# Preparation of the token mixers in pools of their own, ahead of the embedding block

## The chip, the cores and the metric

One Trainium2 chip, one of its cores. The time is device microseconds from start to end of one execution of the whole program; the median of several runs is given. A core has five engines with queues of their own: TensorE (PE, matmuls), VectorE (DVE), ScalarE (ACT), GpSimd (POOL) and SyncE (SP, here only for starting transfers).

## The reference

One step of a four-layer streaming encoder on 256 prompt tokens and 64 sample tokens (320 columns, `NT`), model width 1024, float32. The mixers of the layers are: latent attention (layer 0), stick-breaking attention (1), sliding-window attention (2), latent attention (3). Per layer:

```
x += mixer(rms_norm(x, g_mix))          # with caches of past keys and values for the sample
x += conv_ffn(rms_norm(x, g_ffn))       # 1024 -> 2 x 2816 -> conv of 3 tokens, gelu, gate -> 1024
x += sigmoid(rms_norm(x, g_ple) @ w_gate) * (p[i] @ w_proj)      # the embedding block
```

and a last `rms_norm`. The new keys, values, latents and conv states are outputs too. The caches depend on no layer's result: latents and rotary keys of 256 past tokens, stick-breaking keys and values of 256, window keys and values of 128.

## The kernel before

Everything lies transposed: a feature tile is 128 partitions by 320 token columns. Each float32 operand of PE is kept as a rounded high part and a low part, the remainder, and each product is three matmuls (`mm3`, L190 to L193): high x high, low x high, high x low. `split` (L147 to L150) makes the two parts: ACT copies to the rounded type, DVE (or POOL) subtracts.

The weights are one stream of 450 chunks of eight 128x128 tiles, in the order of use. `fetch` (L157) starts a chunk's transfer on SP's queue, then ACT makes `whi` and DVE `wlo`; inside a mixer every second (window attention: every third) chunk's `wlo` goes to POOL (`wpool`, L164). `take` keeps two chunks ahead (`WAHEAD`); raw chunks have 3 buffers, split chunks 4. Layer 0 takes chunks 0 to 122, layer 1 to 230, layer 2 to 326, layer 3 to 449; a fetch runs two chunks ahead of the use.

A norm is spread over the code: `norm_piece` (L286 on) makes x·g in two parts and adds up the squares, chunk by chunk, as x becomes final; `norm_finish` sums over the partitions with PE (`col_sums`, L261), makes the factor with eleven small DVE steps (`newton_rsqrt`, L241 to L247), and spreads it over the partitions with DVE (L271, L272), PE (L276) and ACT (L279: the tile R). Products with x·g can start before; their results are multiplied by R as they leave PSUM. PSUM has 3 banks for "mm", 3 for "sc", 2 for "tp".

`run` opens a pool `mix{i}` per mixer and a pool `ffn{i}` for `ffn_ple`, the feed-forward part and the embedding block. Each pool takes the memory of the one closed before it. A pool that is opened over a closed one waits, at its first use, for all of the closed one's work. The mixers begin with preparation that needs no x: `mla` loads the rotary table, the cached latents `ckt` and the rotary keys, splits them, clears tiles; `sba` loads the constants `cst`, clears the block-diagonal query tiles `BD`, and per head pair loads and splits a cache `kc`; `swa` loads its rotary table, and in `keys` and `vals` its caches.

The order of instructions on each engine is not the order of the code: a planner that simulates the engines takes, among the instructions whose inputs are ready in its simulation, the earliest in the code. On the chip every engine then goes through its queue in that fixed order, and an instruction that waits holds up all behind it.

Of the kernel before, what the change touches and what calls it, by code (L numbers as in the profile page):

```python
# [8 lines left out]
F32 = mybir.dt.float32  # L9
# [3 lines left out]
ALU = mybir.AluOpType  # L13
# [34 lines left out]
# Order of the 64 rotary features on the partitions: halves interleaved by 16,  # L48
# so that a rotation partner lies in the same quadrant of 32 partitions.
# [55 lines left out]
class Kernel:  # L105
# [16 lines left out]
    # -- small helpers --  # L122
# [29 lines left out]
    # -- weights --  # L152
# [4 lines left out]
    def fetch(self, c):  # L157
# [6 lines left out]
        e = nc.gpsimd if self.wpool and c % self.wpool == 0 else nc.vector  # L164
# [3 lines left out]
    def take(self, name, rows, cols):  # L168
        """The next 128x128 weight tile of the stream, as (high, low) parts."""
# [10 lines left out]
    def take_wide(self, name, rows, cols):  # L180
        """Several tiles of the stream side by side."""
# [13 lines left out]
    def proj(self, out, name, cols, xs, rows=None):  # L195
        """out[cols, tokens] = W[:, cols]^T x over the K tiles xs."""
# [13 lines left out]
    # -- constants, inputs --  # L210
# [54 lines left out]
    def spread(self, r, pool, tag, bufs=2):  # L265
        """A [128, 3] column per token, to every partition: [128, NT]."""
# [19 lines left out]
    def norm_piece(self, m):  # L286
        """Chunk m of x is final: its squares, and x*g in two parts."""
# [47 lines left out]
    # -- the feed-forward block and the per-layer embedding --  # L335
    def ffn_ple(self, i, pool, after):
        nc, tc = self.nc, self.tc
# [3 lines left out]
        pT = self.tile(pool, [P, 2, NT], "pT")  # L341
        nc.sync.dma_start(out=pT, in_=self.t["pT"][i])
        a = []
        for j in range(NF):
# [3 lines left out]
            # gate with the two earlier tokens: zeros and prompt, conv state and sample  # L348
# [29 lines left out]
        ph = self.tile(pool, [P, 2, NT], "pTh", F32R)  # L378
        pl = self.tile(pool, [P, 2, NT], "pTl", F32R)
# [3 lines left out]
        self.norm_start(f"g_ple{i}", pool, "ph")  # L383
        for m in range(NK):
            p = self.ps(("mm", "sc")[m % 2])
            self.proj(p[:, 0:NT], f"fout{i}", np.arange(m * P, m * P + P), a)
            self.add_x(m, p, True)
        h = self.norm_finish(pin=PINS[4])
# [26 lines left out]
    # -- rotary embedding of psum (scaled already if src is SBUF) --  # L415
# [16 lines left out]
    # -- multi-head latent attention --  # L432
    def mla(self, j, pool):
# [8 lines left out]
        flat = lambda x: x.rearrange("p a b -> p (a b)")  # L442
        tmp2, krt, *tmp = (flat(T([P, 2, 3 * P], f"PT{x}", bufs=2)) for x in "hlhl")
        krt = krt[:, 0:W]
        tmp = [x[:, o:o + NT] for x in tmp for o in (0, NT)]
        ckt = T([P, 2, W], "ckt")
        q = nc.sync
        q.dma_start(out=ckt[:, :, NT:W], in_=t["ckvT"][j])
        q.dma_start(out=krt[:, NT:W], in_=t["krT"][j])
# [920 lines left out]
```

## Time and profile before

| | |
|---|---|
| median of 3 runs | 1863.24 us (1861.02 to 1864.79) |
| profiled execution | span 1860.9 us; the time around the span is not given |
| PE busy | 1787.0 us, 12352 matmuls |
| DVE, ACT, POOL busy | 1349.1, 973.4, 568.1 us |
[...]
| transfers | 254.15 MB, mean 137 GB/s |

The span is the time from the first to the last instruction. "Idle before" an instruction is the time for which its engine had nothing running, with the instruction that ended the wait. Matmuls overlap in their engine, so a matmul's duration is longer than the distance to the next.

### The profile page before, as it was taken

How to read it: one execution, taken by the hardware profiler on the slowest of the kernel's cores; microseconds unless marked ns; L12 is line 12 of the kernel's file. 1: busy time of each engine (PE TensorE's matmuls, PEld its weight loads, DVE VectorE, ACT ScalarE, POOL GpSimd, SP SyncE). 2: the span in 40 equal slices, each digit the busy share in tenths (PEclk: the TensorE clock that was granted, in tenths of full speed). 3: DMA queues.
4: the chain of work that ended last, by engine and by line, in shares of the span. 5: the costliest groups of instructions: out<-in, count | busy, mean ns of one | idle time of the engine just before them, and what ended most of it. 6: DMA issues, size and time to landing. Idle time of an engine off the chain costs nothing.

```text
span 1860.9 us, 32664 instructions
## 1 busy us (share of the span) xinstructions
PE 1787.0 (96%) x12352; PEld 1768.3 (95%) x12352; DVE 1349.1 (72%) x2627; ACT 973.4 (52%) x1841; POOL 568.1 (31%) x834
## 2 busy tenths in 40 slices
PE   7999999999989999999997999999979999999996
PEld 6899999999989999999997999999979999999996
DVE  7977687764778888774589787764778777877546
ACT  5776654433558854444457654433547675444332
POOL 3333343321132234330045143321243334333103
PEclk9999999999989999999998999999989999999998
DMA  6333344444443334444352144444432333444441
GB/s 210 106 110 121 121 137 165 152 149 147 148 147 131 126 132 148 148 157 150 125 181 80 58 148 162 147 153 147 138 123 98 128 126 129 150 148 158 149 147 63
DMA packets 78126, 254.15 MB, mean 137 GB/s; under 512 B 9488, under 2 KB 18192, under 8 KB 77968
## 3 DMA queue, kind: packets, MB, share of 16 engines
q1 hardware_dynamic: 77248, 251.34, 38.9%
q8 instruction: 97, 1.59, 0.3%
q10 hardware_dynamic: 720, 0.71, 0.1%
q14 instruction: 61, 0.50, 0.1%
HBM read 243.55 MB, written 5.85 MB: 134 GB/s over the span
## 4 chain that ended last, share of the span: by engine, by line
PE 85%; DVE 7%; ACT 4%; issue 2%; DMA 1%; POOL 1%; DVEq 0%; SPq 0%; ACTq 0%; POOLq 0%
PE ps L191 27%; PE ps L192 27%; PE ps L193 27%; ACT whi L163 1%; DVE wlo L165 1%; DVE rsh L546 1%; DMA wraw<-w 1%; ACT Pr L625 1%; PE ps L645 1%; PE ps L261 0%; PE ps L592 0%; PE ps L593 0%; DVE nb L623 0%; PE ps L1065 0%; PE ps L276 0%
## 5 line engine op out<-in xcount | busy, mean ns | idle before, releaser
L163 ACT ACTIVATE whi<-wraw 128x1024 fp32r<-128x1024 f32 x450 | 474.1, 1056 | 432.5 <-PE ps L192 220.7
L165 DVE TENSOR_TENSOR wlo<-wraw,whi 128x1024 fp32r<-128x1024 f32 x381 | 472.8, 1241 | 228.2 <-ACT whi L163 221.8
L165 POOL TENSOR_TENSOR wlo<-wraw,whi 128x1024 fp32r<-128x1024 f32 x69 | 166.8, 2418 | 287.5 <-ACT whi L163 275.5
L368 POOL TENSOR_TENSOR ge<-cv,R 128x256 f32<-128x256 f32 (+1 forms) x176 | 132.9, 774 | 92.6 <-ACT cv L365 92.2
L309 POOL TENSOR_TENSOR acc<-acc,sq 128x320 f32<-128x320 f32 x72 | 77.4, 1074 | 260.7 <-ACT sq L303 259.8
L331 DVE TENSOR_TENSOR x<-x,ps 128x320 f32<-128x320 f32 x128 | 61.2, 483 | 53.4 <-PE ps L193 53.1
L363 DVE SCALAR_TENSOR_TENSOR cv<-G,cols,cv 128x322 f32<-128x322 f32 x176 | 96.0, 553 | 2.4
L372 DVE TENSOR_TENSOR af<-ge,ps 128x320 f32<-128x320 f32 x88 | 42.8, 486 | 67.7 <-POOL ge L368 67.4
L191 PE MATMUL ps<-h0hi,whi 128*128 128x320 f32 x256 | 81.5, 319 | 8.0 <-ACT h0hi L294 6.5
L191 PE MATMUL ps<-h4hi,whi 128*128 128x320 f32 x256 | 79.9, 314 | 1.1 <-ACT h4hi L149 1.1
L192 PE MATMUL ps<-h0lo,whi 128*128 128x320 f32 x256 | 80.1, 313 | 0.8 <-DVE h0lo L295 0.8
L192 PE MATMUL ps<-h5lo,whi 128*128 128x320 f32 x256 | 79.5, 311 | 1.2 <-DVE h5lo L150 1.2
L192 PE MATMUL ps<-h3lo,whi 128*128 128x320 f32 x256 | 80.3, 314 | 0.0
L191 PE MATMUL ps<-h2hi,whi 128*128 128x320 f32 x256 | 80.2, 313 | 0.0
L192 PE MATMUL ps<-h2lo,whi 128*128 128x320 f32 x256 | 80.2, 313 | 0.0
L191 PE MATMUL ps<-h3hi,whi 128*128 128x320 f32 x256 | 80.1, 313 | 0.0
L193 PE MATMUL ps<-h3hi,wlo 128*128 128x320 f32 x256 | 80.1, 313 | 0.0
L191 PE MATMUL ps<-h1hi,whi 128*128 128x320 f32 x256 | 80.0, 312 | 0.0
L193 PE MATMUL ps<-h1hi,wlo 128*128 128x320 f32 x256 | 79.9, 312 | 0.0
L192 PE MATMUL ps<-h1lo,whi 128*128 128x320 f32 x256 | 79.9, 312 | 0.0
L193 PE MATMUL ps<-h0hi,wlo 128*128 128x320 f32 x256 | 79.9, 312 | 0.0
L193 PE MATMUL ps<-h2hi,wlo 128*128 128x320 f32 x256 | 79.8, 312 | 0.0
(793 smaller groups left out, 6516.3 us busy)
## 6 DMA issues: line engine op xcount, KB each, us to landing
wraw<-w SPq DMA_DIRECT2D x450, 512.0 KB, 3.2
QR<-rsh SPq DMA_DIRECT2D x32, 80.0 KB, 2.0
kc<-sbc SPq DMA_DIRECT2D x8, 256.0 KB, 3.0
x<-xT SPq DMA_DIRECT2D x8, 160.0 KB, 4.1
pT<-pT SPq DMA_DIRECT2D x4, 320.0 KB, 3.3
o_sbk<-kvf SPq DMA_DIRECT2D x8, 160.0 KB, 1.8
o_sbv<-kvf SPq DMA_DIRECT2D x8, 160.0 KB, 1.8
cossin<-rot SPq DMA_DIRECT2D x3, 384.0 KB, 3.2
```

The lines of the kernel that those rows point to most:

```text
L163: nc.scalar.activation(out=hi, in_=raw, func=AF.Copy)
L165: e.tensor_tensor(out=lo, in0=raw, in1=hi.bitcast(F32), op=ALU.subtract)
L191: mm(out, w[0], x[0], start=first, stop=False, **kw)
L192: mm(out, w[0], x[1], start=False, stop=False, **kw)
L193: mm(out, w[1], x[0], start=False, stop=last, **kw)
L309: e.tensor_tensor(out=self.nacc[:, 0:NT], in0=self.nacc[:, 0:NT], in1=sq, op=ALU.add)
L331: self.nc.vector.tensor_tensor(out=self.x[m], in0=self.x[m], in1=p[:, 0:NT], op=ALU.add)
L363: nc.vector.scalar_tensor_tensor(out=cv, in0=gt[:, k:k + GW - 2], scalar=w[k], in1=cv, op0=ALU.mult, op1=ALU.add)
L368: nc.gpsimd.tensor_tensor(out=ge[:, c], in0=cv[:, c.start + o:c.stop + o], in1=R[:, c], op=ALU.mult)
L372: nc.vector.tensor_tensor(out=af, in0=ge, in1=pu[:, 0:NT], op=ALU.mult)
L546: nc.vector.tensor_tensor(out=lo[r, :].bitcast(F32R), in0=qf[r, :], in1=hi, op=ALU.subtract)
L625: nc.scalar.activation(out=pr[:, dst], in_=p[:, src], func=AF.Exp, bias=nb[:, q:q + 1], scale=sc[:, c:c + 1], accum_out=su[:, q:q + 1])
```

## The change

The preparation of each mixer becomes a function of its own (`mla_prep`, `sba_prep`, `swa_prep`), called by `prep`, with a pool `prep{i}`. `run` calls it for the next layer between the feed-forward part and the embedding block, which are now two functions (`ffn`, `ple`); for the first layer it is called right after the first norm pieces. The tiles that the embedding block needs (`pT`, its parts, the norm's tiles, `G2`) go to a pool `ple{i}` at the other end of the memory. The four kinds of pool are opened with `reuse_waits="tile"`: a tile waits for the tiles whose memory it takes, not for the whole closed pool.

In detail: the latent mixer's cached rotary keys get a tile `krc` and are split apart from the new ones (256 columns in `mla_prep`, 320 in `mla`, before 576 in one), and two of the three value blocks are transposed and split in `mla_prep`. In the stick-breaking mixer the first pair's `start`, the constants and the clearing move. In the window mixer `kf` and `vf` get a tile per pair instead of two shared buffers, cached columns are split and cached values transposed in `swa_prep`, and `keys` and `vals` split 320 columns and three blocks instead of 448 and four. POOL takes a chunk's `wlo` only from the fourth chunk fetched after a mixer's start.

```diff
+    def open(self, name, side="left"):
+        c = self.tc.tile_pool(name=name, bufs=1, side=side, reuse_waits="tile")
+        return c, c.__enter__()
...
-        e = nc.gpsimd if self.wpool and c % self.wpool == 0 else nc.vector
+        e = nc.gpsimd if self.wpool and c >= self.wpool_from and c % self.wpool == 0 else nc.vector
...
+    def mla_prep(self, j, pool):
+        self.load_rot(pool)
...
+        ckt, krc = T([P, 2, W], "ckt"), T([P, PAST], "krc")
+        q.dma_start(out=ckt[:, :, NT:W], in_=t["ckvT"][j])
+        q.dma_start(out=krc, in_=t["krT"][j])
...
         self.split(KT[0][:, :, NT:W], KT[1][:, :, NT:W], ckt[:, :, NT:W])
+        self.kr_split(KRh, KRl, krc, slice(NT, W))
+        V = pair([P, 3, KVL], "V")
+        for b in (1, 2):
+            self.latent_turn(V, ckt, b)
+        return ckt, KT, KRh, KRl, V
+
+    def kr_split(self, KRh, KRl, src, c):
+        nc = self.nc
+        nc.scalar.activation(out=KRh[:, c], in_=src, func=AF.Copy)
+        for h in range(2):
+            r = slice(64 * h, 64 * h + 64)
+            nc.vector.tensor_tensor(out=KRl[h][r, c], in0=src[r, :], in1=KRh[r, c].bitcast(F32), op=ALU.subtract)
+
+    def latent_turn(self, V, ckt, b):
+        c = (S0 - 64, NT, NT + P)[b]
+        p = self.ps("tp")
+        for m in range(2):
+            self.nc.tensor.transpose(p[:, m * P:(m + 1) * P], ckt[:, m, c:c + P], self.ident)
+        self.split(V[0][:, b], V[1][:, b], p[:, 0:KVL])
...
+        self.kr_split(KRh, KRl, krt, slice(0, NT))
+        self.latent_turn(V, ckt, 0)
...
+    def sba_prep(self, j, pool):
         BD = [pair([P, 2, NT + DEC], f"BD{b}") for b in range(2)]
...
+        first = start(0)
+        cst = T([P, 4, P], "cst")
+        nc.sync.dma_start(out=cst, in_=t["cst"].rearrange("p (a b) -> p a b", a=4))
+        cr = T([P, 4, P], "cstr", F32R)
+        nc.scalar.activation(out=cr, in_=cst, func=AF.Copy)
+        self.zeros = T([P, PAST], "zeros")
+        nc.gpsimd.memset(self.zeros, 0.0)
+        for b in range(2):
+            for x in BD[b]:
+                nc.gpsimd.memset(x[64:P, 0, 0:NT].bitcast(F32), 0.0)
...
+        return start, first, cr
...
-            if n == 0:
-                start(r)
+            if r not in st:
+                st[r] = start(r)
...
+    def swa_prep(self, j, pool):
+        for kt in range(2):
+            kf, vf = T([P, W], f"kf{kt}"), T([P, W], f"vf{kt}")
+            nc.sync.dma_start(out=kf[:, NT:W], in_=t["wkT"][kt])
+            nc.sync.dma_start(out=vf[:, NT:W], in_=t["wvT"][kt])
...
+        self.load_rot(pool)
+        for kt in range(2):
+            kh = [pair([P, W], f"K{kt}{u}") for u in range(2)]
+            for u in range(2):
...
+                self.split(kh[u][0][s, NT:], kh[u][1][s, NT:], KF[kt][s, NT:])
+            vh = pair([P, 4, P], f"V{kt}")
+            tp = self.ps("tp")
+            nc.tensor.transpose(tp[:, 0:P], VF[kt][:, NT:W], self.ident)
+            self.split(vh[0][:, 3], vh[1][:, 3], tp[:, 0:P])
...
+    def prep(self, i):
+        kind, j = MIXERS[i]
+        c, pool = self.open(f"prep{i}")
+        if self.first and kind == 1:
+            self.later()
+        return c, (self.mla_prep, self.sba_prep, self.swa_prep)[kind](j, pool)
...
+        prep = self.prep(self.layers[0])
         for n, i in enumerate(self.layers):
...
+            c, pool = self.open(f"mix{i}")
+            self.wpool, self.wpool_from = WPOOL[kind], self.wgot + 3
+            (self.mla, self.sba, self.swa)[kind](j, pool, prep[1])
+            self.wpool = 0
+            self.shut(c)
+            self.shut(prep[0])
...
+            cp, ple = self.open(f"ple{i}", "right")
+            c, pool = self.open(f"ffn{i}")
+            e = self.ffn(i, pool, ple)
+            self.shut(c)
...
+                prep = self.prep(self.layers[n + 1])
+                self.ple(i, ple, e, lambda: self.norm_start(f"g_mix{self.layers[n + 1]}"))
+            self.shut(cp)
```

## Rows read from the trace of the kernel before

**Rows 1.** The page, part 1: busy us, share of the span, instructions.
```profile
PE 1787.0 (96%) x12352; PEld 1768.3 (95%) x12352; DVE 1349.1 (72%) x2627; ACT 973.4 (52%) x1841; POOL 568.1 (31%) x834
```

**Rows 2.** Windows: busy us and count by engine, clock, DMA share, GB/s.
```profile
475.00:513.00 38.00, 38.00 (x262) 37.88 (x261) 31.40 (x58) 19.76 (x33) 8.78 (x8) 1.00 0.41 139
...
520.00:540.00 20.00, 12.42 (x63) 11.33 (x62) 15.28 (x33) 8.50 (x15) 4.83 (x2) 0.74 0.47 156
980.00:1040.00 60.00, 48.58 (x339) 46.31 (x338) 53.86 (x179) 44.23 (x143) 25.47 (x29) 0.89 0.17 60
1350.00:1390.00 40.00, 29.12 (x163) 28.00 (x162) 27.10 (x64) 15.38 (x27) 17.10 (x16) 0.79 0.35 122
```

**Rows 3.** Timeline, PE, stick-breaking start: start us, duration us, instruction, idle before.
```profile
516.61 0.72 PE L261 MATMUL ps<-ones,acc 128*128 128x2 f32 x6
...
523.00 0.31 PE L193 MATMUL ps<-h7hi,wlo 128*128 128x320 f32 x1
...
532.15 0.64 PE L191 MATMUL ps<-h0hi,whi 128*128 128x320 f32 x1 [1.05 <-DVE qf L829]
```

**Rows 4.** Timeline, the other engines, same stretch.
```profile
517.46 0.63 ACT L797 ACTIVATE cstr<-cst 128x512 fp32r<-128x512 f32 x1 [3.00 <-DMA cst<-cst]
...
518.48 0.43 DVE L150 TENSOR_TENSOR KTl<-kc,KTh 128x256 fp32r<-128x256 f32 x1 [3.38 <-ACT KTh L149]
...
520.24 0.15 DVE L322 TENSOR_SCALAR ncol<-ps 128x3 f32<-128x3 f32 x1
...
521.81 2.47 POOL L165 TENSOR_TENSOR wlo<-wraw,whi 128x1024 fp32r<-128x1024 f32 x1 [4.33 <-ACT whi L163]
521.96 2.34 DVE L245 TENSOR_TENSOR ncol<-ncol 128x3 f32<-128x3 f32 x1
...
531.13 0.44 ACT L279 ACTIVATE R<-ps 128x320 f32<-128x320 f32 x1 [3.77 <-PE ps L276]
```

**Rows 5.** Timeline, all engines, the norm in the embedding block of layer 0.
```profile
479.04 0.16 DVE L322 TENSOR_SCALAR ncol<-ps 128x3 f32<-128x3 f32 x1
...
481.21 0.65 DVE L271 TENSOR_SCALAR sq<-ident,ncol 128x128 fp32r<-128x128 f32 x3
...
483.53 0.42 ACT L279 ACTIVATE R<-ps 128x320 f32<-128x320 f32 x1
...
491.68 0.31 PE L191 MATMUL ps<-ph0hi,whi 128*128 128x320 f32 x1
```

**Rows 6.** Timeline, all engines, start of the second latent mixer.
```profile
1351.03 0.72 PE L261 MATMUL ps<-ones,acc 128*128 128x2 f32 x6
...
1353.15 0.63 ACT L149 ACTIVATE KTh<-ckt 128x512 fp32r<-128x512 f32 x1 [4.29 <-DMA ckt<-ckvT]
...
1354.42 0.15 DVE L322 TENSOR_SCALAR ncol<-ps 128x3 f32<-128x3 f32 x1
...
1356.36 2.50 DVE L472 TENSOR_TENSOR PTh<-PTh,PTh 128x320 f32<-128x320 f32 x1
...
1357.41 0.31 PE L193 MATMUL ps<-h7hi,wlo 128*128 128x320 f32 x1
...
1360.80 2.30 DVE L246 SCALAR_TENSOR_TENSOR ncol<-ncol,ncol 128x3 f32<-128x3 f32 x1
...
1364.04 0.63 PE L276 MATMUL ps<-sq,negones 128*128 128x320 f32 x1 [6.31 <-DMA wraw<-w]
...
1377.13 2.80 DVE L487 TENSOR_TENSOR KR<-PTl,KR 64x576 fp32r<-64x576 f32 x2
...
1381.13 0.90 PE L496 MATMUL ps<-ident,ckt 128*128 128x128 f32 x3 [3.40 <-DVE ckt L478]
```

**Rows 7.** Groups of instructions, line 165: count, busy us, mean ns, idle before.
```profile
L165 DVE TENSOR_TENSOR wlo<-wraw,whi 128x1024 fp32r<-128x1024 f32 x381 | 472.8, 1241 | 228.2 <-ACT whi L163 221.8
L165 POOL TENSOR_TENSOR wlo<-wraw,whi 128x1024 fp32r<-128x1024 f32 x69 | 166.8, 2418 | 287.5 <-ACT whi L163 275.5 <-DVE PTh L472 12.0
```

**Rows 8.** Timeline, DVE, start of the first latent mixer.
```profile
20.35 1.61 DVE L325 TENSOR_SCALAR nv<-ncol 128x3 f32<-128x3 f32 x1
```

More of the change, by code (lines that the diff above doesn't have):

```diff
@@ L333, in add_x, with ffn @@
             self.norm_piece(m)
-    def ffn_ple(self, i, pool, after):
-        nc, tc = self.nc, self.tc
+    def ffn(self, i, pool, ple):
+        nc = self.nc
         h = self.norm_finish(pin=PINS[3])
@@ L340, in ffn_ple @@
         stage = self.tile(pool, [P, NF, 4], "stage")
-        pT = self.tile(pool, [P, 2, NT], "pT")
+        pT = self.tile(ple, [P, 2, NT], "pT")
         nc.sync.dma_start(out=pT, in_=self.t["pT"][i])
@@ L387, in ffn_ple, with ple @@
             self.add_x(m, p, True)
+        return ph, pl
+    def ple(self, i, pool, p_emb, after):
+        nc = self.nc
+        ph, pl = p_emb
         h = self.norm_finish(pin=PINS[4])
@@ L455, in mla @@
         self.split(KT[0][:, :, NT:W], KT[1][:, :, NT:W], ckt[:, :, NT:W])
+        self.kr_split(KRh, KRl, krc, slice(NT, W))
[4 more added lines that the diff above has]
+    def kr_split(self, KRh, KRl, src, c):
+        nc = self.nc
+        nc.scalar.activation(out=KRh[:, c], in_=src, func=AF.Copy)
[8 more added lines that the diff above has]
+        self.split(V[0][:, b], V[1][:, b], p[:, 0:KVL])
+    def mla(self, j, pool, prep):
+        nc, t = self.nc, self.t
+        W = NT + PAST
+        T = lambda shape, tag, dt=F32, bufs=1: self.tile(pool, shape, tag, dt, bufs)
+        pair = lambda shape, tag, bufs=1: self.pair(pool, shape, tag, bufs)
+        ckt, KT, KRh, KRl, V = prep
+        flat = lambda x: x.rearrange("p a b -> p (a b)")
+        tmp2, krt, *tmp = (flat(T([P, 2, 3 * P], f"PT{x}", bufs=2)) for x in "hlhl")
+        krt = krt[:, 0:NT]
+        tmp = [x[:, o:o + NT] for x in tmp for o in (0, NT)]
         h = self.norm_finish(keep_sum=True, pin=PINS[0])
@@ L482, in mla @@
         nc.vector.tensor_tensor(out=kr, in0=kv[2], in1=R, op=ALU.mult)
-        self.rotate(pool, kr, krt[:, 0:NT])
-        nc.scalar.activation(out=KRh, in_=krt, func=AF.Copy)
-        for h_ in range(2):
-            r = slice(64 * h_, 64 * h_ + 64)
-            nc.vector.tensor_tensor(out=KRl[h_][r, :], in0=krt[r, :], in1=KRh[r, :].bitcast(F32), op=ALU.subtract)
-        nc.sync.dma_start(out=t["o_ckv"][j], in_=ckt[:, :, 0:NT])
-        nc.sync.dma_start(out=t["o_kr"][j], in_=krt[0:64, 0:NT])
-        blocks = [S0 - 64, NT, NT + P]
-        V = pair([P, 3, KVL], "V")
-        for b, c in enumerate(blocks):
-            p = self.ps("tp")
-            for m in range(2):
-                nc.tensor.transpose(p[:, m * P:(m + 1) * P], ckt[:, m, c:c + P], self.ident)
-            self.split(V[0][:, b], V[1][:, b], p[:, 0:KVL])
+        self.rotate(pool, kr, krt)
+        self.kr_split(KRh, KRl, krt, slice(0, NT))
+        nc.sync.dma_start(out=t["o_ckv"][j], in_=ckt[:, :, 0:NT])
+        nc.sync.dma_start(out=t["o_kr"][j], in_=krt[0:64, :])
+        self.latent_turn(V, ckt, 0)
         qacc = tmp2[:, NT + DEC:2 * (NT + DEC)]
@@ L780, in mla @@
             self.norm_piece(m)
-    def sba(self, j, pool):
+    def sba_prep(self, j, pool):
         nc, t = self.nc, self.t
@@ L817, in start, with sba @@
             self.split(V[0][:, 3:5], V[1][:, 3:5], kc[:, 1].rearrange("p (a b) -> p a b", a=2))
-            st[r] = BD[r % 2], KT, V
+            return BD[r % 2], KT, V
+        first = start(0)
[8 more added lines that the diff above has]
+                nc.gpsimd.memset(x[64:P, 0, 0:NT].bitcast(F32), 0.0)
+                nc.gpsimd.memset(x[0:64, 0, NT:].bitcast(F32), 0.0)
+                nc.gpsimd.memset(x[0:64, 1, 0:SEQ].bitcast(F32), 0.0)
+        return start, first, cr
+    def sba(self, j, pool, prep):
+        nc, t = self.nc, self.t
+        W = NT + PAST
+        T = lambda shape, tag, dt=F32, bufs=1: self.tile(pool, shape, tag, dt, bufs)
+        pair = lambda shape, tag, bufs=1: self.pair(pool, shape, tag, bufs)
+        start, first, cr = prep
+        identr, tri, mdiag = (cr[:, n] for n in range(3))
+        mown = cr[:, 3, 0:DEC]
+        h = self.norm_finish(pin=PINS[1])
+        R = self.R
+        O = []
+        st = {0: first}
         def project(r, n, tag="mm"):
-            if n == 0:
-                start(r)
+            if r not in st:
+                st[r] = start(r)
             bd, KT, V = st[r]
@@ L1021, in vals @@
             nc.sync.dma_start(out=t["o_wv"][kt], in_=vf)
-            vh = pair([P, 4, P], f"V{kt}")
-            pv = four(transposes([vf[:, c:c + P] for c in (0, P, S0 - 64, NT)]))
-            self.split(vh[0], vh[1], pv)
-            V.append(vh)
+            pv = transposes([vf[:, c:c + P] for c in (0, P, S0 - 64)])[:, 0:3 * P]
+            self.split(vh[0][:, 0:3], vh[1][:, 0:3], pv.rearrange("p (a b) -> p a b", a=3))
         st = {}
```

82 lines of the change are left out of this document (30 added, 52 removed).

## The prediction

> **What bounds the kernel now.** I read the page first, then the ten-us windows, then the timeline of each stretch in which a window was not full. [...] The windows show where that is [rows 2]. In the embedding block (475 to 513 us) PE is full: 262 matmuls in 38.00 us, 0.145 us each. At the start of the stick-breaking mixer (520 to 540) there are 63 in 20 us where 138 would fit: 75 x 0.145 = 10.9 us lost, at a granted clock of 0.74. At the start of the second latent mixer (1350 to 1390) there are 163 for 276, some 16.4 us lost (a little less in truth, as some of them are shorter), clock 0.79. In the window-attention mixer (980 to 1040) PE idles 11.4 us, but there VectorE (DVE) is busy 53.86 of 60 us.
>
> The two starts have one shape. PE sums the squares of the norm (L261, done at 516.61 + 0.72 = 517.33), goes on with the four projections that PSUM has room for, runs out at 523.31 and resumes at 532.15 [rows 3]: 8.8 us. It waits for the norm's factor R. DVE could begin that chain at 517.4 and begins at 520.24 [rows 4]: in its queue the split of the cached keys (KTl) stands ahead, which waits for ScalarE (ACT), which stands still for 3.00 us for the `cst` transfer. All these tiles lie in a pool that opens over the feed-forward pool only when the embedding block is done with it, so transfer, copy and split begin at the moment when the norm is due. Then two things stretch the chain: R is ready at 531.13 + 0.44 = 531.57, 11.3 us after its first step, while the same chain in the embedding block takes from 479.04 to 483.95, 4.9 us [rows 5]. One is that while GpSimd (POOL) ran a weight split, 521.81 to 524.28, a DVE instruction on 3 columns took 2.34 us, of which all but its 0.16 is standing still [rows 4]; the other are DVE's own weight splits, 1.24 us each [rows 7]. In the second latent mixer it is ACT that waits 4.29 us for `ckt`, the chain starts at 1354.42 instead of 1351.75, is stopped twice by POOL splits (2.50 and 2.30 us), and PE stands from 1357.72 to 1364.04; later it stands 3.40 us for the keys [rows 6].
>
> **The change, part by part.** (a) *Preparation ahead of the embedding block.* Transfers of caches, constants and rotary tables, their splits, the clearing of tiles and the transposes of cached values go into a pool of their own, traced before the block. Its memory lies over the feed-forward activations, free once the last output product is done, about 475 us; PE starts the mixer 35 us later. The slowest such wait here was 4.7 us from issue to use (ckt, the 4.29 that ACT waited and a little before), so it lands long before it is due.
>
> *Stick-breaking start.* The chain begins at 517.3. With the 4.9 us of the embedding block R is there at 522.2, before PE runs out (523.3): nothing is lost, gain 10.9. With one DVE split (1.24) and one POOL split (2.3) still in it R comes at 525.8 and its first use 0.5 later: a stop of 3.0, and if the clock falls as now another 2.1 (10.9 - 8.8): 5.1 lost, gain 5.8. I take 8, between the two; lower end 4, if what stands in the embedding block delays the last chunk of the norm by some 2 us.
>
> *Second latent mixer, first stop.* The chain starts at 1351.75. To the end of L271 it needs 2.8 bare (479.04 to 481.86), plus two DVE splits 2.5, the sum of squares 0.5 (its 2.50 without the lock), one POOL lock 2.1: 1359.7, against PE's 1357.7. A stop of 2.0 for 6.3, and part of the slow restart: I take 6. Ends: 2.7 (only the 1354.42 - 1351.75 moves, both locks stay) and 9 (stop and restart both go).
> *Second stop.* The split of the rotary keys that takes 2.80 us covers 576 columns and will cover 320; by columns (an estimate) 1.2 us less. Two of three blocks of value transposes leave the queue. With the 3.40 shortened, 3 us including some clock; ends 0 (another thing is late by as much) and 5.8.
>
> *Window attention.* PE never waits for R there. The splits lose 128 of 448 columns, two input transfers leave the shared buffers. DVE is the limit, so 1 us; ends -2 and 4 (a third of its 11.4).
>
> *First layer.* Nothing precedes it, so preparation is only reordered: cached rotary keys and two blocks of values are split early, when DVE is full and the chain runs. I count 0: the 1.61 us that one 3-column step takes there under POOL's split [rows 8] should shrink, some 1.7 us of splits (four, at the 0.43 us of one of 256 columns [rows 4]) come in. Ends -2 and +2.
>
> (b) *Waits by tile.* They are what lets (a) start at 475 instead of after the block; by themselves they delete waits and add none. Feed-forward starts are not limited by pool waits, so 0.
>
> (c) *Fewer POOL splits.* `wpool_from` keeps the first three chunks fetched in a mixer on DVE. Counting chunks (123 + 108 + 96 + 123), those that change engine are 4, 126, 234 and 330, four of 69 [rows 7]: each costs DVE 1.24 and saves it a stop of up to 2.3. In the last three layers they lie at the end of the embedding block, in front of the norm's last chunks, so the chain begins up to 1 us sooner, which the terms above may contain; I add nothing. But 128, 332 and 334 stay on POOL, and those are the ones that stop the chains now.
>
> [...]
>
> (d) *What the embedding block pays.* Per block there are added on DVE two to six splits (0.43 us per 256 columns [rows 4], 1 to 3 us in all), as much on ACT, up to 768 KB of transfers ahead of weight chunks on SP's queue, a few PE transposes (0.1 us each). DVE is busy 31.4 of 38 us there, so it has 6.6 us of room [rows 2]. If ACT waits for a transfer as it did in the mixers (3 to 4.3 us), the block's own R, ready at 483.95, comes that much later; the PSUM bank that it frees is next needed at 491.68 [rows 5], so up to 7 us are hidden. Should that cover fail, PE stops for what exceeds it. I charge 1 us for all three; ends 0 and 4.5.
>
> Sum: 8 + 6 + 3 + 1 + 0 - 1 = 17 us. The profiled execution has a span of 1860.9 us; its own time is not given beside it, but the runs' median is 1863.24, 2.3 us above, and I carry that difference unchanged: 1863.2 - 17 = 1846.
>
> **The rivals.** *The locks keep the chains long.* POOL splits 128, 332 and 334 fall into the earlier chains as they do now, DVE's own queue fills the rest, and only the 2.9 and 2.7 us of late start are won, with little of the clock: 4 + 2.7 + 0 + 0 - 0 = about 7, so 1856. For it: the chains were stretched more by these (6.4 us) than by the start. Against: their timing is set by PE's progress, and in the block itself the chain ran undisturbed.
> *Both stops vanish whole.* R arrives before PE runs out in both mixers: 10.9 + 9 + 5.8 + 2 = 28, 1835. Against: the same locks.
> *Nothing moves.* The preparation is traced earlier but reaches the engines late, or the planner's new order takes back elsewhere (the latent mixers stop for 0.3 to 2 us in many places) what the starts give: 1862. Against: the tiles are free 35 us ahead, and DVE has room.
> *Slower: SP's queue blocks the weights.* The preparation's transfers stand in SP's one queue in front of weight chunks and wait for the activations' release or for one another. PE eats a chunk of 8 tiles in 24 x 0.145 = 3.5 us and two chunks are ready ahead, so it decides from 7 us of blocked queue; each us beyond costs one, and each stop about 2 us of clock. With 14 us in each of three blocks that is 3 x (7 + 2) = 27, less the 17: 1873. For it: in the mixers these transfers did take 4 to 6 us. Against: three of them overlap and land within about 5 us.
>
> **How the numbers follow.** Forecast 0.58 (own range 1839 to 1853), locks 0.20, both whole 0.06, nothing moves 0.08, slower 0.08. The range takes in the locks rival and the low bounds: 1835 to 1860. A difference under 0.2% (3.7 us) cannot be told from none here: faster than 1859.5 are the first three with most of their width, 0.82; within it 0.09; slower 0.09.
>
> **What would show it.** Right: the KTl, cstr and KTh copies of the mixers at 478 to 500 and their counterparts; no ACT wait for `cst` or `ckt` after the block; the chain's first step within 0.5 us of L261's end; stops of at most 3 us at both starts; the clock there near 0.95; four POOL splits fewer. Wrong: PE no longer full in the embedding block; 2 us steps in every chain as now (the locks rival); weight copies on ACT waiting for their transfers in the block (the slower one). A gain that sits in the window-attention mixer, or a loss in the first layer, would mean I looked in the wrong place.

## The result and the profile after

The changed kernel took 1871.7 us (median of 5 runs, 1867.96 to 1874.12), the kernel before 1863.18 beside it; the ratio on record is 1.0052, 95% interval 1.0037 to 1.0067. It is 8.5 us slower by the medians, and outside the range of 1835 to 1860, where 17 us less were forecast. The profiled execution has a span of 1870.7 us for 1860.9.

From the page of the changed kernel, busy time of each engine, beside [rows 1]:

```profile
PE 1793.6 (96%) x12352; PEld 1773.6 (95%) x12352; DVE 1349.8 (72%) x2641; ACT 975.3 (52%) x1849; POOL 558.6 (30%) x830
```

TensorE (PE) runs the same 12,352 matmuls, is busy 6.6 us longer, and stands still 77.1 us for 73.9. The windows of the changed kernel, of three of the stretches of [rows 2], columns as there, the granted clock as a share of full speed:

```profile
475.00:513.00 38.00, 37.70 (x258) 37.34 (x257) 31.20 (x60) 21.59 (x38) 5.40 (x7) 1.00 0.54 176
520.00:540.00 20.00, 14.91 (x85) 14.06 (x83) 13.77 (x31) 7.19 (x13) 4.89 (x2) 0.83 0.37 122
1350.00:1390.00 40.00, 33.16 (x204) 32.16 (x203) 30.43 (x68) 16.38 (x28) 14.68 (x15) 0.90 0.40 133
```

The two starts look better than before, 85 matmuls for 63 and 204 for 163 (they begin 4 and 11 us earlier in the work, so both gains are overstated), and the sum is still worse. Windows at fixed times slide against the work, so I compare by matmuls: each kernel here has 12,352, and the start of the n-th can be set against that of the n-th in the other. By that measure the changed kernel loses 3.8 us in the first mixer (to matmul 1590), 0.6 in the first embedding block, gains 2.7 at the stick-breaking start (3480 to 3620), loses 0.8 up to the end of the second block, 7.1 in the window mixer (6340 to 7163), 1.4 in the third block, and gains 0.7 over the second latent mixer (8937 to 10611). That is 10.3; 0.5 comes back at the end: 9.8, the difference of the spans.

*Stick-breaking start.* Timeline of the changed kernel, to be held against [rows 3] and [rows 4] (start us, duration us, instruction, in brackets the idle time before it):

```profile
479.58 0.43 DVE L159 TENSOR_TENSOR KTl<-kc,KTh 128x256 fp32r<-128x256 f32 x1 [0.34 <-ACT KTh L158]
479.94 0.63 ACT L837 ACTIVATE cstr<-cst 128x512 fp32r<-128x512 f32 x1
...
521.46 0.72 PE L270 MATMUL ps<-ones,acc 128*128 128x2 f32 x6
522.23 0.16 DVE L331 TENSOR_SCALAR ncol<-ps 128x3 f32<-128x3 f32 x1 [3.38 <-PE ps L270]
522.50 1.23 DVE L174 TENSOR_TENSOR wlo<-wraw,whi 128x1024 fp32r<-128x1024 f32 x1
523.46 2.53 POOL L174 TENSOR_TENSOR wlo<-wraw,whi 128x1024 fp32r<-128x1024 f32 x1 [7.29 <-ACT whi L172]
523.64 2.37 DVE L254 TENSOR_TENSOR ncol<-ncol 128x3 f32<-128x3 f32 x1
527.14 1.22 DVE L174 TENSOR_TENSOR wlo<-wraw,whi 128x1024 fp32r<-128x1024 f32 x1
528.67 2.73 DVE L280 TENSOR_SCALAR sq<-ident,ncol 128x128 fp32r<-128x128 f32 x3
528.79 2.36 POOL L174 TENSOR_TENSOR wlo<-wraw,whi 128x1024 fp32r<-128x1024 f32 x1 [2.80 <-ACT whi L172]
531.45 0.41 PE L285 MATMUL ps<-sq,negones 128*128 128x320 f32 x1 [3.73 <-DVE sq L280]
533.86 0.63 PE L200 MATMUL ps<-h0hi,whi 128*128 128x320 f32 x1 [1.05 <-DVE qf L870]
```

The preparation is where it was forecast, 40 us ahead, and the chain's first step follows the norm sums at once (522.18, 522.23). But two weight splits of VectorE (DVE) and two of GpSimd (POOL) stand in the chain; under POOL's, a 3-column step takes 2.37 us instead of 0.16 and three small products 2.73 instead of 0.65 (0.15 and 0.65 in sba8 below, where POOL's splits begin with the ninth chunk). A step of over 2 us beside a POOL split is what the prediction and the expectations call a lock; what holds it up no run shows. The sums are done at 522.18 and PE resumes at 533.86: 11.7 us, where it was 14.8 before.

*Second latent mixer*, answering to [rows 6]:

```profile
1363.01 0.72 PE L270 MATMUL ps<-ones,acc 128*128 128x2 f32 x6
1365.32 2.40 POOL L174 TENSOR_TENSOR wlo<-wraw,whi 128x1024 fp32r<-128x1024 f32 x1 [7.78 <-DVE wlo L174]
1365.43 2.31 DVE L255 SCALAR_TENSOR_TENSOR ncol<-ncol,ncol 128x3 f32<-128x3 f32 x1
1370.34 2.34 POOL L174 TENSOR_TENSOR wlo<-wraw,whi 128x1024 fp32r<-128x1024 f32 x1 [2.62 <-ACT whi L172]
1370.48 2.64 DVE L280 TENSOR_SCALAR sq<-ident,ncol 128x128 fp32r<-128x128 f32 x3
1373.17 0.64 PE L285 MATMUL ps<-sq,negones 128*128 128x320 f32 x1 [3.91 <-DVE sq L280]
1388.93 0.47 PE L482 MATMUL ps<-ident,ckt 128*128 128x128 f32 x1 [2.32 <-DVE ckt L519]
```

The same picture: a timely start, two stops under POOL's splits (2.31 us for a step of 0.16, 2.64 for three of 0.65 together), PE waits 3.91 us for 6.31 and later 2.32 for 3.40.

*First mixer.* Of the kernel before and then of the changed one, the norm sums and what stands on DVE ahead of the chain:

```profile
19.39 0.72 PE L261 MATMUL ps<-ones,acc 128*128 128x2 f32 x6
```

```profile
19.41 0.75 DVE L159 TENSOR_TENSOR Vl<-ps,Vh 128x256 fp32r<-128x256 f32 x2
20.07 2.35 DVE L174 TENSOR_TENSOR wlo<-wraw,whi 128x1024 fp32r<-128x1024 f32 x2
23.03 0.72 PE L270 MATMUL ps<-ones,acc 128*128 128x2 f32 x6
23.79 0.16 DVE L331 TENSOR_SCALAR ncol<-ps 128x3 f32<-128x3 f32 x1 [1.37 <-PE ps L270]
```

On DVE the value splits of the preparation and two weight splits go first. On PE the sums are the 90th to 95th matmul where they were the 69th to 74th, and run 3.6 us later; PE's stop behind them is 4.27 us for 3.34.

*Embedding blocks.* In the second and third the preparation's last split holds up the block's own norm sums, by 0.52 and 1.23 us, here the third. In the first, where 0.6 us are lost, DVE begins the norm's chain 0.6 us after the sums, behind the preparation's splits, and PE stops for 0.30 us. The transfers don't hold PE up: the longest wait of ScalarE (ACT) in a block that the profile puts down to one is 2.3 us, and PE waits for none.

```profile
1324.13 0.83 PE L270 MATMUL ps<-ones,acc 128*128 128x2 f32 x6 [1.23 <-DVE Vl L159]
```

*Window mixer.* In its second half in the changed kernel, all of PE's stops up to the one in which the granted clock fell, and the windows before and after that fall:

```profile
1019.68 0.39 PE L200 MATMUL ps<-K10h,Qh 128*128 128x256 f32 x1 [0.61 <-ACT Pr L1111]
1024.28 0.71 PE L200 MATMUL ps<-O0h,whi 128*128 128x320 f32 x3 [0.39 <-ACT O0h L158]
1026.04 0.66 PE L1126 MATMUL ps<-ident,Pr 128*128 128x128 f32 x4 [0.44 <-DVE O0l L159]
1030.85 0.63 PE L1126 MATMUL ps<-ident,Pr 128*128 128x128 f32 x4 [0.42 <-DVE PTl L159]
1034.61 0.33 PE L200 MATMUL ps<-K10h,Qh 128*128 128x128 f32 x1 [0.41 <-ACT Pr L1111]
1037.83 0.55 PE L200 MATMUL ps<-PTh,V0h 128*128 128x256 f32 x1 [1.00 <-DVE O0l L159]
...
1016.70:1037.10 20.40, 17.74 (x134) 15.97 (x132) 17.48 (x77) 16.74 (x66) 2.35 (x6) 1.00 0.00 1
1037.10:1047.40 10.30, 8.88 (x37) 8.68 (x38) 5.11 (x19) 4.80 (x18) 0.00 (x0) 0.50 0.01 2
```

Five stops of at most 0.61 us and a sixth of 1.00; within the sixth the clock falls to 0.50, and 37 matmuls run in the next 10.3 us. None of these waits is for something that the change moved: the mixer's own instructions stand in another order.

### The profile page after: what moved, and what is told of

Same layout as the page of the kernel before. It is cut to its first block, busy times and chain, and to the rows that moved or that the text cites. A ratio compares the mean times of both kernels' runs of the same rounds, so it can differ in the third digit from the quotient of the medians.

```text
span 1870.7 us, 32639 instructions
## 1 busy us (share of the span) xinstructions
PE 1793.6 (96%) x12352; PEld 1773.6 (95%) x12352; DVE 1349.8 (72%) x2641; ACT 975.3 (52%) x1849; POOL 558.6 (30%) x830
## 4 chain that ended last, share of the span: by engine, by line
PE 86%; DVE 9%; ACT 3%; issue 1%; DMA 0%; POOL 0%; DVEq 0%; SPq 0%; ACTq 0%
PE ps L200 28%; PE ps L201 27%; PE ps L202 27%; DVE wlo L174 1%; ACT whi L172 1%; PE ps L676 1%; DVE rsh L577 1%; PE ps L270 1%; ACT Pr L656 0%; PE ps L623 0%; DVE rc L1062 0%; PE ps L624 0%; DVE sq L280 0%; DVE PTl L159 0%; DVE m L1103 0%
## 5 line engine op out<-in xcount | busy, mean ns | idle before, releaser
L174 DVE TENSOR_TENSOR wlo<-wraw,whi 128x1024 fp32r<-128x1024 f32 x385 | 478.6, 1244 | 222.1 <-ACT whi L172 215.9
L174 POOL TENSOR_TENSOR wlo<-wraw,whi 128x1024 fp32r<-128x1024 f32 x65 | 156.9, 2413 | 312.8 <-ACT whi L172 295.8
```

The lines of the kernel that those rows point to most:

```text
L174: e.tensor_tensor(out=lo, in0=raw, in1=hi.bitcast(F32), op=ALU.subtract)
```

## The experiments

In this table each column is a stretch as above, in us against the kernel before, from one profiled execution each; W is the window mixer from norm sums to norm sums (125.2 us before). Stretches in which nothing was changed and TensorE's order is that of before still scatter: the first mixer by -3.7 to +0.8, the second latent one by -1.1 to +0.8, the stick-breaking start by -1.1 to 0, W by 0.5. The ratio is to the kernel before on the same chip; the stretches are held against the one profiled execution of the kernel before.

| kernel | first mixer | stick-br. start | W, us | blocks | second latent | ratio (95%) |
|---|---|---|---|---|---|---|
| changed | +3.8 | -2.7 | 131.6 | +2.7 | -0.7 | 1.0052 (1.0037, 1.0067) |
| c_alone | -0.9 | -2.4 | 129.7 | 0 | -0.2 | 1.0021 (1.0011, 1.0032) |
| no_c | +1.9 | -2.9 | 129.5 | +3.3 | -0.9 | 1.0030 (1.0018, 1.0041) |
| in_place | +4.3 | -3.5 | 127.3 | +0.8 | +1.2 | 1.0037 (1.0024, 1.0049) |
| late0 | -2.3 | -3.5 | 133.7 | +3.0 | -0.5 | 1.0031 (1.0022, 1.0041) |
| sba_alone | -0.9 | -3.4 | 125.5 | +0.7 | -2.1 | 0.9969 (0.9956, 0.9981) |
| swa_alone | +0.8 | -0.7 | 133.6 | +0.7 | +0.8 | 1.0064 (1.0051, 1.0076) |
| c_2 | -0.5 | -0.1 | 130.1 | 0 | -0.9 | 1.0039 (1.0024, 1.0054) |
| mla3_alone | -1.3 | -0.3 | 125.2 | +1.2 | -1.9 | 0.9991 (0.9982, 1.0000) |
| swa_load | -1.0 | -0.2 | 125.3 | 0 | +0.5 | 1.0004 (0.9994, 1.0015) |
| sba8 | -2.2 | -4.3 | 124.8 | +0.6 | -1.1 | 0.9993 (0.9983, 1.0004) |
| sba_mla3 | -3.7 | -3.6 | 125.5 | +2.4 | -0.8 | 0.9993 (0.9983, 1.0002) |
| sba_mla3_8 | -3.8 | -4.4 | 125.7 | +1.9 | -8.1 | 0.9951 (0.9937, 0.9965) |
| best1 | -5.2 | -3.6 | 130.1 | +3.4 | -8.6 | 0.9963 (0.9951, 0.9976) |
| locks0 | -6.4 | -0.1 | 130.5 | 0 | -7.8 | 0.9967 (0.9956, 0.9978) |
| best_pin3 | -6.2 | -7.1 | 131.1 | +6.4 | -8.6 | 0.9953 (0.9940, 0.9967) |
| l10 | +0.1 | -1.1 | 125.2 | 0 | -6.0 | 0.9969 (0.9957, 0.9981) |
| c0_10 | +0.3 | -3.6 | 125.5 | +1.8 | -8.8 | 0.9954 (0.9942, 0.9966) |
| p3_10 | -2.6 | -8.6 | 125.5 | +1.7 | -10.2 | 0.9914 (0.9900, 0.9929) |

**Parts taken out or alone.** c_alone is the kernel before with part (c); no_c the changed kernel without it:

```diff
-        e = nc.gpsimd if self.wpool and c % self.wpool == 0 else nc.vector
+        e = nc.gpsimd if self.wpool and c >= self.wpool_from and c % self.wpool == 0 else nc.vector
```

> The kernel before with only the later start of POOL's weight splits (the first three chunks fetched in a mixer stay on DVE). Theory A (the loss is the scheduler's new order in stretches that the change did not have to touch, and the moved preparation pays at the starts): within 3 us of the kernel before, 1860 to 1866. Rival C (fewer POOL splits put DVE's own weight splits into the chains, above all two of 1.2 us ahead of the first layer's norm and in the window mixer): 1867 or more, with the first layer's norm sums at 22 us or later instead of 19.4.

> The changed kernel with POOL's weight splits from the mixer's first chunk again, as before the change. Theory A: within 3 us of the changed kernel, 1869 to 1875. Rival C: 1866 or less, with the first layer's 3.8 us back.

Part (c) alone costs 4.0 us by the median, where theory A had at most 3, and taking it out saves 4 by the ratios, to 1867.17 us, between the two forecasts: it is not neutral, as I had counted it. The first layer is not where: its sums stand at 19.1 us in c_alone, so rival C is wrong there; the window mixer is, 129.7 us for 125.2. And c_alone gains 2.4 us at the stick-breaking start with nothing prepared ahead; no_c, with the preparation alone, gains 2.9 there and the changed kernel, with both, 2.7: the two don't add.

in_place issues the preparation after the embedding block, late0 puts the first layer's splits back:

```diff
-                prep = self.prep(self.layers[n + 1])
+                ahead = self.layers[n + 1] in ()
+                if ahead:
+                    prep = self.prep(self.layers[n + 1])
                 self.ple(i, ple, e, lambda: self.norm_start(f"g_mix{self.layers[n + 1]}"))
             self.shut(cp)
+            if not last and not ahead:
+                prep = self.prep(self.layers[n + 1])
```

```diff
-        self.kr_split(KRh, KRl, krc, slice(NT, W))
+        if not self.first:
+            self.kr_split(KRh, KRl, krc, slice(NT, W))
...
-        for b in (1, 2):
+        for b in () if self.first else (1, 2):
...
+        if self.first:
+            self.kr_split(KRh, KRl, krc, slice(NT, W))
...
-        self.latent_turn(V, ckt, 0)
+        for b in range(3 if self.first else 1):
+            self.latent_turn(V, ckt, b)
```

> The changed kernel with the preparation of layers 1 to 3 issued after the embedding block, at the mixer's start; all else as changed. Theory A: the 3 us of the stick-breaking start and the 6 us of the second latent mixer's start go, the window mixer and the bodies move by what their order gives, either way by up to 7: about 1880, and no less than 1873. Rival B (the preparation costs the embedding blocks 3 us and the window mixer 7 us wherever it stands ahead): those 10 us come back against the 9 that go, about 1870, with the window mixer's 131 us from norm to norm back at 125.

> The changed kernel with the first layer's cached rotary keys and value blocks 1 and 2 split at their old places, after the new keys. Theory A: the first layer's norm sums are back at about 19.4 us from 23.0 and the 3.8 us there come back, 1868, unless a new order elsewhere takes it. Rival C: the two DVE weight splits ahead of the norm are the cause, so nothing comes back: 1871 to 1873.

in_place did not undo what it was to undo, and its 1867.65 us missed both forecasts. Its timeline shows the copies in the block all the same:

```profile
480.43 0.43 DVE L159 TENSOR_TENSOR KTl<-kc,KTh 128x256 fp32r<-128x256 f32 x1 [0.68 <-ACT KTh L158]
```

So the place of the call does not bring the work forward. What is left is memory that is free early and the waits by tile, which no run takes apart, and this run says nothing on A or B. late0 brings the sums to 20.3 us and the first mixer from +3.8 to -2.3, beyond the scatter: the early splits were the cause, those of the value blocks, as the scheduler (the planner that orders the queues) still ran those of the rotary keys at 16.2 us. The window mixer took 2 us of it back, though its PE instructions stand exactly as in the changed kernel: there the granted clock stood at 0.50 for 27.3 us in place of 20.5. One order of PE can thus differ by 2 us in W.

**One mixer's preparation at a time.** Here the other mixers are those of the kernel before, and so is POOL. c_2 moves nothing but one weight split:

```diff
+            if not last and self.layers[n + 1] in (1,):      # sba_alone; (2,): swa_alone; (3,): mla3_alone
                 cp, ple = self.open(f"ple{i}", "right")
...
+            else:
+                c = tc.tile_pool(name=f"ffn{i}", bufs=1)
```

```diff
-            self.wpool = WPOOL[kind]
+            self.wpool, self.wpool_from = WPOOL[kind], self.wgot + 3 if kind in (2,) else 0      # c_2
```

> The kernel before, with the stick-breaking mixer's preparation alone moved ahead (its own pool, waits by tile, POOL's splits as before). Theory A (the preparation pays at its mixer's start, and the losses are the new order elsewhere): 3.1 us less at the start, 0.6 to 0.8 us more in the embedding block ahead of it, the rest as before: 2 to 3 us faster than the kernel before. Rival B (preparation ahead costs as much as it brings): 0 +- 1 us. My forecast before the change was 8 us for this part.

> The kernel before, with the window-attention mixer's preparation alone moved ahead. Theory A: no gain at its start, 0.7 us of block, and the mixer, 125.2 us from norm to norm before, comes out where its new order and TensorE's clock put it, 127 to 134 us as in the other kernels: 2 to 9 us slower than the kernel before, the same kind of loss as in the next kernel, which prepares nothing. Rival B: the preparation's early instructions are the cost, 7 us, and the next kernel costs nothing.

> The kernel before with one weight split, number 234 at the end of the embedding block ahead of the window-attention mixer, on DVE instead of POOL; no preparation is moved. Theory A: the order that the scheduler makes of the mixer changes with it and costs some 5 us, as with all such splits moved (4.9 us there): 5 us slower than the kernel before. Rival B: the mixer stays at 125 us and the kernel within 1 us of the one before.

> The kernel before, with the second latent mixer's preparation alone moved ahead. Theory A: the first stop shrinks by 6 us, of which 5 are given back by 1440 us in later stops and clock, and the embedding block pays 1.4 us: 0 to 1 us slower than the kernel before. Rival (the give-back in the changed kernel came from elsewhere): 4 to 6 us faster.

The stick-breaking part brings 3.4 less 0.7 us by the stretches, as theory A had it, and more by the ratio (0.31%, some 6 us): 2.1 us of it stand in the second latent mixer, which the scheduler had re-ordered too, the rest in the scatter of other stretches. The second latent part lies between its two forecasts: 0.09% faster, 0 to 0.18. The window part costs 9.4 us by the stretches and 12 by the ratio, above the 2 to 9 expected. c_2 shows that this loss needs no preparation: one split of 1.2 us, before the mixer begins, goes to DVE, and W is 130.1. But the two lose their time in different ways. W of the kernel before, of the changed one and of c_2:

```profile
954.80:1080.00 125.20, 112.91 (x792) 110.03 (x792) 107.56 (x281) 83.09 (x222) 53.61 (x58) 0.95 0.29 100
958.00:1089.60 131.60, 115.99 (x787) 112.20 (x786) 109.86 (x281) 83.07 (x222) 55.02 (x55) 0.92 0.27 90
954.55:1084.67 130.12, 112.37 (x789) 108.98 (x788) 110.30 (x281) 83.16 (x222) 54.63 (x55) 0.95 0.27 92
```

In c_2 PE is busy no longer than before, at the same mean clock, and stands still 5.5 us more; in the changed kernel it stands still 3.3 us more and is busy 3.1 us longer, at a mean clock of 0.92 for 0.95.

**The window mixer: moved work or new order?** swa_load moves only its transfers ahead:

```diff
-            kh = [pair([P, W], f"K{kt}{u}") for u in range(2)]
...
-            vh = pair([P, 4, P], f"V{kt}")
...
+                self.split(kh[u][0][s, :], kh[u][1][s, :], kf[s, :])
...
+            pv = four(transposes([vf[:, c:c + P] for c in (0, P, S0 - 64, NT)]))
```

> The kernel before, with only the window-attention mixer's transfers (cached keys and values, rotary tables) moved ahead into buffers of their own; clearing, splits and transposes stay in the mixer, all 448 columns. The order of the mixer's instructions is then nearly that of before. Theory A (the loss is the new order of the mixer's DVE and PE work): mixer 124 to 126 us from norm to norm, kernel within 2 us of before. Rival B (what is moved ahead costs in itself): 2 us slower or more.

W is 125.3. Its stops in the half shown above for the changed kernel, and the window of the same length from 1014.1 us, when the clock had come back:

```profile
1015.08 0.39 PE L200 MATMUL ps<-K10h,Qh 128*128 128x256 f32 x1 [0.35 <-ACT Pr L1104]
1025.07 0.39 PE L200 MATMUL ps<-K10h,Qh 128*128 128x256 f32 x1 [0.51 <-ACT Pr L1104]
1033.78 0.66 PE L1119 MATMUL ps<-ident,Pr 128*128 128x128 f32 x4 [1.04 <-DVE O0l L159]
...
1014.10:1044.80 30.70, 28.52 (x221) 27.28 (x220) 26.84 (x106) 25.81 (x95) 1.32 (x3) 1.00 0.05 18
```

Three stops for six, and the clock stays at 1.00: 221 matmuls run in 30.7 us, for 134 and 37. Over all kernels W has two groups: 124.8 to 125.7 in the ten (the kernel before among them) in which PE's order of the mixer differs from that of before in two places at most, and 127.3 to 133.7 in the ten in which it differs in six or more, from 62 us into the mixer at the latest. best1, locks0 and best_pin3 are in the second group and change nothing in this mixer nor right before it.

**POOL's splits in the chains.** sba8 starts POOL's splits in the stick-breaking mixer with the ninth chunk, sba_mla3 moves two preparations and leaves POOL, sba_mla3_8 does both:

```diff
-            self.wpool = WPOOL[kind]
+            self.wpool, self.wpool_from = WPOOL[kind], self.wgot + 8 if kind in (1,) else 0      # sba8; sba_mla3_8: (0, 1)
+            if not last and self.layers[n + 1] in (1,):      # sba8; sba_mla3, sba_mla3_8: (1, 3)
```

> The stick-breaking preparation alone moved ahead, and in that mixer POOL's weight splits from the ninth chunk fetched on, so that none falls into the norm's chain. Theory of the locks: the chain from norm sums to the first use of R, 12 us with preparation ahead, loses two stops of 2.2 and 2.1 us and takes up to two more DVE splits of 1.24: 9.5 to 10.5 us, and the kernel is 2 to 3 us faster than with the preparation alone, 8 us faster than before in all, unless the window mixer's order changes. Rival (the stops are not the limit; DVE's own splits fill the place): within 1 us of the preparation alone.

> The stick-breaking and the second latent mixer's preparation moved ahead, the first layer and the window mixer as before, POOL's splits as before. If the parts add: 2.7 us and 1 to 2 us, some 4 us faster than the kernel before by the stretches, up to 7 by the medians of the two kernels alone. If a move changes what comes after it: the window mixer off 125 us, and no gain.

> The same two preparations ahead, and POOL's weight splits from the ninth chunk on in the first, second and fourth mixers; the window mixer's as before. Theory of the locks: all three norm chains lose their 2 us stops, 2 us each less 1.24 for each split that DVE takes over: 3 to 6 us faster than with the two preparations alone. Rival (DVE, which is busy 40 of 50 us at the latent mixers' starts, pays): equal or up to 4 us slower than those.

In sba8 the start of the sums and the first use of R are 10.5 us apart for 12.4, as the theory of the locks had it, but the mixer's body, in a new order too, gives back 2.4 by its end: no gain in all, where 2 to 3 us over the preparation alone were expected. sba_mla3_8 gives back 2.9 there. The two preparations add in the stretches, and by the medians bring nothing that can be told (0.9983 to 1.0002). In the second latent mixer the later start of POOL's splits decides: -8.1 us for -0.8.

Is the preparation needed there? best1 has both preparations and locks0 none; in both POOL starts with the ninth chunk in the latent mixers alone:

```diff
+            self.wpool, self.wpool_from = WPOOL[kind], self.wgot + 8 if kind in (0,) else 0
```

> The stick-breaking and second latent preparations ahead, POOL's weight splits from the ninth chunk on in the two latent mixers alone; the stick-breaking and window mixers keep POOL's splits as before. Expected from the stretches: the second latent mixer 8 us faster as in the kernel with both mixers' splits moved, the stick-breaking mixer 3.4 us faster at its start and without the 3 us that it gave back in its body there: 0.5 to 0.7% faster than the kernel before, 1849 to 1851 where that has 1861. If the give-back in the body came from the latent mixers' splits: no better than that kernel, 0.5%.

> The kernel before with nothing prepared ahead; only POOL's weight splits of the two latent mixers begin with the ninth chunk. Theory of the locks with the preparation needed: the second latent mixer's chain still starts 2.7 us late behind the ckt transfer, so of the 8 us at most 5 are gained there. Rival (the stops under POOL's splits were all of it): 7 us or more faster in that mixer, and the preparation is worth nothing there.

> As the first of these kernels, with the stick-breaking mixer's third projection kept behind the norm sums on TensorE, so that the sums don't wait in TensorE's queue after their input is ready (DVE stood 3.4 us there in the changed kernel). If that queueing is part of the stop: its chain begins 1 to 2 us sooner and the kernel is 1 to 3 us faster than the first. If not, within 1 us of it, or slower by what TensorE idles before the sums.

locks0 gains 7.8 us in that mixer with nothing prepared ahead, though with a new order of it: the rival was right. ACT still waits for `ckt`, and PE's stop is 1.88 us for 6.31:

```profile
1350.66 0.63 ACT L158 ACTIVATE KTh<-ckt 128x512 fp32r<-128x512 f32 x1 [3.67 <-DMA ckt<-ckvT]
1358.38 0.42 PE L285 MATMUL ps<-sq,negones 128*128 128x320 f32 x1 [1.88 <-DVE sq L280]
```

best1 misses its forecast because W went to 130.1. best_pin3 (its edit is `PINS[1] = {3: 0}`: in PE's queue the third projection comes only after the norm sums) gains 3.5 more at the start and loses 3.0 more in the blocks.

**A version that is faster.** With the eleventh chunk instead of the ninth the scheduler leaves the window mixer alone. l10 prepares nothing, c0_10 adds the two preparations, p3_10 the pin:

```diff
-            self.wpool, self.wpool_from = WPOOL[kind], self.wgot + 8 if kind in (0,) else 0
+            self.wpool, self.wpool_from = WPOOL[kind], self.wgot + 10 if kind in (0,) else 0
...
-PINS = ({5: 2}, {}, {}, {}, {6: 0, 7: 1, 8: 1})
+PINS = ({5: 2}, {3: 0}, {}, {}, {6: 0, 7: 1, 8: 1})
```

> Nothing prepared ahead; POOL's weight splits of the two latent mixers begin with the eleventh chunk instead of the ninth, a start at which the scheduler keeps the window mixer's order of the kernel before. Theory A (the window mixer's second half has two orders, and the one of before costs 125 us, the other 127 to 134): the mixer is back at 125 to 126 us from norm to norm and the kernel some 5 us faster than with the ninth chunk, 0.994 of before. Rival (the window mixer's time is chance from run to run): 130 us again, 0.997.

> The same, with the stick-breaking and the second latent mixer's preparation ahead. If the preparation adds what the stick-breaking start showed (3.4 less 0.7 us) and nothing in the second latent mixer: 2 to 4 us faster than without it, 0.992 of before. If the embedding blocks take it back: equal.

> The same again, with the stick-breaking mixer's third projection kept behind the norm sums. Earlier it took 3.6 us in the embedding block and gave 4.1 more at the start: within 2 us of the kernel without it.

W is 125.2 in l10, as forecast; the kernel is not faster than locks0, since the first mixer lost what the window mixer won. c0_10 against l10 is 0.9954 against 0.9969 with intervals that overlap: what the preparation is worth beside the later splits is not settled by the medians. p3_10 was forecast within 2 us of c0_10 and is 0.4% faster: 1846.33 us, where the kernel before has 1862.67. Why, the two timelines show. c0_10, then p3_10:

```profile
517.43 0.72 PE L270 MATMUL ps<-ones,acc 128*128 128x2 f32 x6
523.30 1.22 DVE L174 TENSOR_TENSOR wlo<-wraw,whi 128x1024 fp32r<-128x1024 f32 x1
525.20 2.89 DVE L281 SCALAR_TENSOR_TENSOR sq<-ident,ncol,sq 128x128 fp32r<-128x128 f32 x3
525.20 2.54 POOL L174 TENSOR_TENSOR wlo<-wraw,whi 128x1024 fp32r<-128x1024 f32 x1 [3.24 <-ACT whi L172]
528.14 0.64 PE L285 MATMUL ps<-sq,negones 128*128 128x320 f32 x1 [2.39 <-DVE sq L281]
...
517.50:537.50 20.00, 15.35 (x89) 14.37 (x88) 15.32 (x33) 9.05 (x15) 5.08 (x2) 0.83 0.39 130
```

```profile
514.48 0.72 PE L270 MATMUL ps<-ones,acc 128*128 128x2 f32 x6
521.19 0.81 DVE L281 SCALAR_TENSOR_TENSOR sq<-ident,ncol,sq 128x128 fp32r<-128x128 f32 x3
521.91 1.22 DVE L174 TENSOR_TENSOR wlo<-wraw,whi 128x1024 fp32r<-128x1024 f32 x1
522.05 0.41 PE L285 MATMUL ps<-sq,negones 128*128 128x320 f32 x1 [0.30 <-DVE sq L281]
522.25 3.14 POOL L174 TENSOR_TENSOR wlo<-wraw,whi 128x1024 fp32r<-128x1024 f32 x1 [3.24 <-ACT whi L172]
...
515.00:535.00 20.00, 18.42 (x122) 17.55 (x123) 16.45 (x37) 14.03 (x27) 5.93 (x3) 1.00 0.51 165
```

The pin did not bring the sums forward, as it was meant to (both kernels have them at the same place in the work). It changed the order on DVE: one weight split of 1.2 us went from ahead of L281 to behind it. In both kernels POOL's second split begins 7.77 us after the sums; in p3_10 L281 is then done, in c0_10 it begins at that moment and takes 2.89 us. PE waits 0.30 us for 2.39, the clock stays at 1.00 for 0.83, and 122 matmuls fit where 89 did: 1.2 us of DVE's queue turned into 5. Of the 10 us between these two profiled executions only those 5 are explained: 2.9 in the first mixer and 1.4 in the second latent one stand in stretches whose PE order is the same in both.

## Why the prediction was wrong

- *Stick-breaking start, gain 8:* 2.7 came. The start was right (the copies at 480, no wait for `cst`, the first step 0.05 us after the sums); the step that failed is "with one DVE split and one POOL split still in it". There were two of each, one more of 1.2 us and one stop of 2.1, and the clock with them (0.83, where 0.95 was named as the sign of being right): that is the rival of the long chains, which had 4 here. p3_10, with one of each, gains 8.6.
- *Second latent mixer, 6 and 3:* 0.7 over the mixer. Of the first stop 2.4 us went, of the second 1.1, and short stops up to 1440 us, with the granted clock behind them (0.91 on the mean from 1390 to 1440 us, 1.00 before), took back most of the rest. Here the cause itself was mis-sized: I charged the late transfer with 2.7 us and POOL's splits with 2.1 that would stay. locks0 shows that without those splits 7.8 us go, the transfer as late as ever.
- *Window attention, gain 1 (-2 to 4):* 7.1 lost, the largest term of the miss. The failed step is the assumption behind each term, that a stretch in which nothing is moved keeps its order and its time; the rival "nothing moves" had the new order, but let it take back only what the starts give. It needs no moved work, as c_2 shows, and moved transfers alone don't cause it, as swa_load does. In the changed kernel PE's stops of over 0.25 us sum to 15.4 us for 11.9; what is left is the clock behind them (0.92 for 0.95). What in the new order makes the stops longer stays open.
- *First layer, 0 (-2 to +2):* 3.8 lost; in late0 the stretch is 6.1 us shorter than that. That the splits come early when DVE is full I had seen, and priced at 1.7 us of splits, not at what the norm sums lose that queue behind them. A loss here was among the prediction's own signs of having looked in the wrong place.
- *Embedding blocks, 1 (0 to 4.5):* 2.7, inside the range: in two blocks the V split ahead of the norm sums, in the first the splits ahead of the norm's chain, not a transfer.
- *Waits by tile, 0:* in_place fits their being what moves the preparation, together with where its memory lies; no run takes them out. *Four splits on DVE:* they are four (65 for 69 on POOL), but not free: by order alone c_2 costs 5 us.
- *The slower rival* named the SP queue. PE is full in the blocks (37.70 of 38.00 us) and waits for no weight there; the kernel is slower for another reason, and that its 1873 us lies next to the 1871.7 measured is luck.

Of the prediction's locks the runs show lengths and no mechanism. Beside a POOL weight split, in the trace after, a 3-column step took 2.31 us in place of 0.16 and three products of one tile and a column of scalars 2.73 in place of 0.65. In sba8, where POOL's splits in the stick-breaking mixer begin with the ninth chunk, the same steps took 0.15 to 0.17 and 0.65. In locks0, with that start in the latent mixers, PE's stop in the second was 1.88 us for 6.31.

## What to carry to other kernels

Where a scheduler lays out every queue, an edit's sum is its own terms and a lottery on every stretch that may be re-ordered: compare the stretches by matmul count, not by the clock, and try variants until the untouched ones keep their order. Read what stands in a chain before asking when it starts: here taking POOL out of the first chunks was worth 6 to 8 us in the second latent mixer (in the first, from nothing to 6), and starting its transfer earlier at most 3. A us on an engine that feeds a stop can be worth five: 1.2 us on DVE were, between c0_10 and p3_10, where a step of 2.89 us for 0.81 beside a POOL split and a granted clock of 0.83 for 1.00 came with them.

## What the runs showed of the hardware

In the traces of both kernels the granted clock stands at 1.00 or at 0.50; its mean is 0.983 before and 0.982 after. In the kernel before, matmuls of 320 columns begin 0.27 us apart at 0.50 (533 to 536 us) and 0.145 us apart at 1.00 (475 to 513 us). The number of short stops did not decide when the clock fell. In the window mixer of the changed kernel it fell to 0.50 after five stops of 0.39 to 0.61 us in 20 us, as a sixth, of 1.00, began; in swa_load it stayed at 1.00 through three (0.35, 0.51, 1.04), and in c_2 through six within 22 us (0.69, 0.92, 0.42, 0.40, 0.99, 0.71):

```profile
1018.00:1040.00 22.00, 17.88 (x143) 16.85 (x141) 17.30 (x71) 15.19 (x56) 0.60 (x2) 1.00 0.00 1
```

What decides it no run here shows. The first mixer, with the same order on PE and DVE in eight kernels, took 241.3 to 245.8 us to its 1590th matmul, on more than one chip, so that one profiled execution tells little of a change of 3 us there.
